# First stage of an encoder layer: only k, v and a quarter of q first, summed in PSUM, and the rest of q inside the attention

## The chip, the core and the metric

The kernel runs on one core of a Trainium2 chip. The metric is the device time of one execution in microseconds (us), median of several runs. Before the change it is 1121.42 us (three runs, 1117.03 to 1121.68). One further execution, recorded by the profiler, took 1123.08 us; its trace spans 1121.3 us from the first to the last instruction. All durations below come from that execution.

## What is computed

One layer of an encoder: 256 tokens of width 2048, everything in fp32. A vector `c` gives, by a matrix of 2048 x 12288, shifts, scales and gates; the input is scaled and shifted by them, goes through a windowed attention with 32 query heads and 8 key heads, a layer norm, and an MLP of width 8192 with a second norm.

```python
c_act = jax.nn.silu(c)
mod = c_act @ mod_w[i] + mod_b[i]
sh_m, sc_m, g_m, sh_f, sc_f, g_f = jnp.split(mod, 6, axis=-1)
hmix = x * (1.0 + sc_m[:, None, :]) + sh_m[:, None, :]
proj = hmix @ w_qkv + b_qkv                      # 2048 x 3072: q 2048, k 512, v 512
q, k = apply_rope(q, cos, sin), apply_rope(k, cos, sin)
s = where(|kpos - qpos| <= 128, q k^T / 8, -inf)
p = exp(s - m) / (sum(exp(s - m)) + exp(sink - m))
y = (p @ v) @ w_o + b_o
x = layer_norm(ALPHA * x + (1 + g_m) * y)
u = square(relu((x * (1 + sc_f) + sh_f) @ w1 + b1))
x = layer_norm(ALPHA * x + (1 + g_f) * (u @ w2 + b2))
```

## The kernel before

**Stream.** Weights come from HBM in chunks of 1 MB (128 x 2048 floats) through one list, `Stream.q`. SyncE issues the loads in the order of the list, into five buffers (`raws`) and, up to the second step of the attention, three more (`raws2`). A matrix chunk is split in two halves: ScalarE rounds each to `wh` (L281), VectorE forms the rest `wl = raw - wh` (L252). Each product of two fp32 tiles is then three matmuls (`mm3`, L560 to L562): xh wh, xh wl, xl wh. A chunk serves 24 matmuls of 128 x 512.

**Modulation.** `mod` chunks are of two kinds. A row chunk is multiplied on TensorE (`Mod.step`, L336); a column chunk is multiplied and summed in one VectorE instruction (`Col.step`, L376). A group of k tiles (`Group`) is turned into columns (`columns`, L405) and then `modulated` (L581) makes the scaled input, split into `hh` and `hl`. The first stage needs 32 such chunks, 18 rows and 14 columns. The list goes on with chunks for the gate and for the MLP's scales (`plan_late`, `SLOT_FILL`).

**First stage.** The 2048 rows of `w_qkv` are taken in six groups of 1, 1, 2, 4, 4 and 4 k tiles (`MIXG`), each over all six column chunks of 512 (k, v and four of q). Since five PSUM banks cannot hold twelve sums, `evict` (L596) copies the first partial sum to SBUF and adds each later one on VectorE (L607). `ORDER`, `CARRY` and `FIRST` are orders written out by hand. 19 of the 24 chunks of `w_qkv` are multiplied before the attention starts, five (`LATE`) in its first five steps.

**Attention.** Sixteen steps n = 0 to 15, one for each pair of key heads, half of the queries and half of the group: `scores` (L744), softmax, `normalise`, in the next step `probs_T`, every second step `values`. Each step also multiplies one matrix chunk: a late one of `w_qkv` in steps 0 to 4, from step 5 (`OUT_AT`) one of `w_o`. After step 15 five steps with a `w_o` chunk alone follow. `project` takes `w_o` in four passes over heads, each ends with an addition to `ys` on VectorE. `rope` and `heads_T` (L730) prepare the next quarter of q every fourth step. After the last chunk the norm follows (`add_gated`, `norm_scalars`, `normed`), its result is transposed (`ff_input`, L985) and the MLP starts (L1055).

**Order.** Each engine runs its instructions in a fixed order; a framework sorts them beforehand and adds the waits. `S.pin` keeps the program's order in the first stage. PSUM's eight banks are in three pools: five for sums, two for transposes, one for row chunks.

Of the kernel before, what the change touches and what calls it, by code (L numbers as in the profile page):

```python
# [20 lines left out]
S = 256  # L21
# [20 lines left out]
FIRST = [[(0, 0), (0, 1), (0, 2), (0, 3)],  # L42
         [(0, 4), (0, 5), (1, 4), (1, 5)],
         [(1, 0), (1, 1), (1, 3), (1, 2)]]
# [27 lines left out]
def hybrid_kernel(ctx: ExitStack, tc: tile.TileContext, a, out: bass.AP):  # L72
# [7 lines left out]
    psa = ctx.enter_context(tc.tile_pool(name="psa", bufs=5, space=PSUM))  # L80
    pst = ctx.enter_context(tc.tile_pool(name="pst", bufs=2, space=PSUM))
    psm = ctx.enter_context(tc.tile_pool(name="psm", bufs=1, space=PSUM))
# [48 lines left out]
    def spread():  # L131

        for c in range(4):
            ps = psa.tile([128, 512], F32, name="pa")
# [184 lines left out]
    class Mod:  # L319
# [24 lines left out]
        def step(self, raw):  # L344
            w, kc, i = self.w, self.kc, self.i
            if i == 0:
                self.ps = psm.tile([128, 512], F32, name="pm")
# [31 lines left out]
    class Group:  # L379
# [25 lines left out]
        def columns(self):  # L405
# [8 lines left out]
            pt = pst.tile([128, 512], F32, name="pt")  # L414
# [8 lines left out]
    class Gate(Group):  # L423
# [15 lines left out]
        def rows(self, m, h):  # L439
            pt = pst.tile([128, 512], F32, name="pt")  # L440
# [9 lines left out]
        def spread(self, g):  # L450
# [3 lines left out]
            pt = pst.tile([128, 512], F32, name="pt")  # L454
# [21 lines left out]

    G = len(MIXG)
    LATE = [(5, 3), (4, 4), (5, 4), (4, 5), (5, 5)]

    ORDER = {2: (1, 0, 2), 3: (5, 4, 3, 0, 2, 1), 4: (1, 2, 3, 0), 5: (0, 1, 2)}  # L480
    CARRY = {((1, 2), 2), ((2, 2), 5), ((3, 1), 1), ((4, 0), 0)}
    CARRY |= {(x, x[1]) for x, y in zip(LATE, LATE[1:]) if x[1] == y[1]}
    qk_order = [(g, c) for g in range(2, G) for c in ORDER[g]]
    wq = lambda g, c: S.plan(a["wqkv"][m_mix[g].k0 * 6 // 4 + c])
    m_mix[0].plan(2)
    S.plan(a["wqkv"][0])
    m_mix[1].plan(2)
    S.plan(a["wqkv"][1])
    S.plan(a["wqkv"][2])

    S.side[len(S.q)] = lambda: load_x(1)
    m_mix[2].plan(3)
    wq(2, ORDER[2][0])
    m_mix[2].plan(1)
    for g in range(2, G):
        n = len(ORDER[g])
        if g + 1 < G:
            S.side[len(S.q)] = lambda g=g: load_x(g)
        for x, c in enumerate(ORDER[g][1:], 1):
            if g + 1 < G:  # L500
                m_mix[g + 1].plan({2: [0, 0, 3], 3: [0, 2, 2, 2, 1, 1], 4: [0, 3, 3, 2]}[g][x])
            wq(g, c)
        if g == 2:
            m_mix[3].plan(4)
        if g + 1 < G:
            wq(g + 1, ORDER[g + 1][0])
        if g == 2:
            m_mix[3].plan(1)
# [10 lines left out]
    OUTS = [(c, js, x) for js in ((0,), (1,), (2,), (3,)) for c in range(4) for x in range(len(js))]  # L519
    for n in range(OUT_AT + 16):  # L520
        plan_late(SLOT_FILL[n])
        if n == X_AT:
            S.side[len(S.q)] = lambda: load_rows()
        if n < len(LATE):
            wq(*LATE[n])
# [55 lines left out]
    def modulated(g):  # L581
        m = m_mix[g]
        m.columns()
        k0, nk = m.k0, m.nk
        hh, hl = g4(F32R), g4(F32R)
        for k in range(nk):
            s = slice(k * 256, k * 256 + 256)
            xt, sc, sh = xts.pop(k0 + k), modm[:, 0, k0 + k:k0 + k + 1], modm[:, 1, k0 + k:k0 + k + 1]
            tc.keep_in_program_order(nc.scalar.activation(hh[:, s], xt, AF.Identity, scale=sc, bias=sh))  # L589
            tc.keep_in_program_order(nc.vector.tensor_scalar(xt, xt, sc, sh, op0=OP.mult, op1=OP.add))  # L590
            tc.keep_in_program_order(nc.vector.tensor_sub(hl[:, s], xt, f32(hh[:, s])))  # L591
        held[g] = hh, hl
# [3 lines left out]
    def evict(c, pss):  # L596

        new = c not in acc
        if new:
            acc[c] = g4()  # L600
        for t in range(NT):
            av = acc[c][:, t * 512:t * 512 + 512]
            if new:
                bq(pss[t], c)
                nc.scalar.copy(av, pss[t])
            else:
                nc.vector.tensor_add(av, av, pss[t])  # L607

    def banks():
        return [psa.tile([128, 512], F32, name="pa") for _ in range(NT)]  # L610

    def qkv_first(n):

        wh, wl = S.main()
        for i, (g, p) in enumerate(FIRST[n]):
            hh, hl = held[g]
            c = CORD[p]
            opens = c not in half
            held_back = ((g, n), p) in CARRY or (n == 1 and g == 0)
            pss = half.pop(c, None) or banks()  # L620
            for t in range(NT):
                s = slice(t * 128, t * 128 + 128)
                mm3(pss[t], hh[:, s], hl[:, s], wh(i), wl(i), opens, c in acc and not held_back)
            if i % 2:
                S.done()
            if held_back:
                half[c] = pss
            else:
                evict(c, pss)
# [623 lines left out]
```

## Time and profile before

| what | us |
| --- | --- |
| median of three runs | 1121.42 |
| profiled execution | 1123.08 |
| its span | 1121.3 |
| first matmul of the first `scores` | 170.24 |
| first matmul of the last `scores` (step 15) | 325.98 |
| last `mm3` of the attention starts | 369.81 |
| first matmul of the MLP (L1055) | 384.26 |
| TensorE / VectorE / ScalarE busy, share of the span | 96% / 71% / 47% |

Busy is not the same as fast: a matmul of 128 x 512 is listed with 0.39 us, while the next one starts 0.23 us after it. How much of a stage is lost is therefore seen from starts and from the idle times that the timeline puts in brackets, with what ended them. The granted clock is 1.0 at full speed and 0.5 when the chip throttles TensorE.

### The profile page before, as it was taken

How to read it: one execution, taken by the hardware profiler on the slowest of the kernel's cores; microseconds unless marked ns; L12 is line 12 of the kernel's file. 1: busy time of each engine (PE TensorE's matmuls, PEld its weight loads, DVE VectorE, ACT ScalarE, POOL GpSimd, SP SyncE). 2: the span in 40 equal slices, each digit the busy share in tenths (PEclk: the TensorE clock that was granted, in tenths of full speed). 3: DMA queues.
4: the chain of work that ended last, by engine and by line, in shares of the span. 5: the costliest groups of instructions: out<-in, count | busy, mean ns of one | idle time of the engine just before them, and what ended most of it. 6: DMA issues, size and time to landing. Idle time of an engine off the chain costs nothing.

```text
span 1121.3 us, 16337 instructions
## 1 busy us (share of the span) xinstructions
PE 1071.7 (96%) x6554; PEld 884.6 (79%) x6554; DVE 799.9 (71%) x1157; ACT 526.8 (47%) x811; POOL 20.3 (2%) x40
## 2 busy tenths in 40 slices
PE   8699999999999699999999999999999999999995
PEld 6578766667777499988888887888888888888884
DVE  2797898887879866765568886766665656665576
ACT  4433337766763445653345543344444434444340
POOL 1000000000000000000000000000000000000001
PEclk9999999998999799999999999999999999999998
DMA  9999998785876788555678787876555555557521
GB/s 384 425 425 427 411 371 338 293 298 198 316 285 226 305 325 326 175 186 191 229 281 294 261 291 251 309 287 218 186 184 192 200 188 188 188 187 264 188 75 75
DMA packets 43652, 292.75 MB, mean 261 GB/s; under 512 B 4876, under 2 KB 5036, under 8 KB 9784
## 3 DMA queue, kind: packets, MB, share of 16 engines
q1 hardware_dynamic: 40400, 281.96, 67.4%
q0 software_dynamic: 2432, 8.41, 2.5%
q10 hardware_dynamic: 744, 1.34, 0.3%
q8 instruction: 51, 0.84, 0.3%
q14 instruction: 25, 0.20, 0.1%
HBM read 289.57 MB, written 2.11 MB: 260 GB/s over the span
## 4 chain that ended last, share of the span: by engine, by line
PE 83%; DVE 8%; DMA 4%; issue 3%; ACT 2%; SPq 0%; POOL 0%; DVEq 0%; POOLq 0%; ACTq 0%
PE pa L1079 16%; PE pa L560 15%; PE pa L561 14%; PE pa L562 14%; PE pa L1080 8%; PE pa L1056 3%; PE pa L1057 3%; PE pa L1055 3%; DMA raw<-in_mod 3%; PE pm L336 3%; DVE raw L376 2%; DVE wl L252 2%; PE pa L753 1%; ACT wh L281 1%; PE pt L792 1%
## 5 line engine op out<-in xcount | busy, mean ns | idle before, releaser
L252 DVE TENSOR_TENSOR wl<-raw,wh 128x1024 fp32r<-128x1024 f32 x332 | 403.0, 1223 | 225.3 <-ACT wh L281 222.7
L281 ACT CAST wh<-raw 128x1024 fp32r<-128x1024 f32 x332 | 347.6, 1050 | 440.3 <-PE pa L562 240.0
L560 PE MATMUL pa<-wh,g 128*128 128x512 f32 x816 | 324.6, 399 | 4.8 <-ACT g L589 2.1
L561 PE MATMUL pa<-wl,g 128*128 128x512 f32 x816 | 321.3, 394 | 2.1 <-DVE wl L252 2.1
L562 PE MATMUL pa<-wh,g 128*128 128x512 f32 x816 | 319.5, 393 | 1.9 <-DVE g L591 1.4
L1079 PE MATMUL pa<-g,wh 128*128 128x512 f32 x768 | 271.6, 399 | 0.0
L1080 PE MATMUL pa<-g,wl 128*128 128x256 f32 x768 | 215.7, 281 | 0.0
L560 PEld LDWEIGHTS pa<-wh,g 128*128 128x128 f32 x816 | 154.4, 189 | 45.5 <-issue 6.2
L562 PEld LDWEIGHTS pa<-wh,g 128*128 128x128 f32 x816 | 154.4, 189 | 36.5 <-DVE g L591 3.0
L561 PEld LDWEIGHTS pa<-wl,g 128*128 128x128 f32 x816 | 154.7, 190 | 35.5 <-DVE wl L252 3.3
L1079 PEld LDWEIGHTS pa<-g,wh 128*128 128x128 f32 x768 | 144.3, 188 | 36.2 <-issue 0.2
L1080 PEld LDWEIGHTS pa<-g,wl 128*128 128x128 f32 x768 | 145.1, 189 | 0.1
L376 DVE CUSTOM_DVE_ANT_0 raw<-raw,cb 128x2048 f32<-128x2048 f32 x54 | 123.4, 2286 | 19.8 <-DMA raw<-in_mod 19.8
L1056 PE MATMUL pa<-g,wh 128*128 128x256 f32 x256 | 73.7, 288 | 0.4 <-DVE g L999 0.4
L1055 PE MATMUL pa<-g,wh 128*128 128x256 f32 x256 | 73.3, 289 | 0.3 <-ACT g L991 0.3
L1057 PE MATMUL pa<-g,wl 128*128 128x256 f32 x256 | 73.1, 286 | 0.0
L336 PE MATMUL pm<-raw,cact 128*32 128x128 f32 (+1 forms) x1216 | 46.5, 289 | 6.0 <-DMA raw<-in_mod 5.7
L1055 PEld LDWEIGHTS pa<-g,wh 128*128 128x128 f32 x256 | 49.8, 196 | 1.1 <-ACT g L991 0.7
L1056 PEld LDWEIGHTS pa<-g,wh 128*128 128x128 f32 x256 | 49.7, 194 | 1.1 <-DVE g L999 0.7
L1057 PEld LDWEIGHTS pa<-g,wl 128*128 128x128 f32 x256 | 49.8, 194 | 0.2 <-issue 0.2
L336 PEld LDWEIGHTS pm<-raw,cact 128*32 128x32 f32 x1216 | 31.7, 110 | 21.6 <-issue 11.2
L770 ACT ACTIVATE g<-g,nm 128x256 f32<-128x256 f32 x64 | 31.8, 498 | 21.3 <-DVE nm L760 21.3
(174 smaller groups left out, 696.4 us busy)
## 6 DMA issues: line engine op xcount, KB each, us to landing
raw<-in_mod SPq DMA_DIRECT2D x96, 1024.0 KB, 7.7
raw<-in_w SPq DMA_DIRECT2D x64, 1024.0 KB, 4.9
raw<-in_w1b SPq DMA_DIRECT2D x48, 1024.0 KB, 4.9
raw<-in_wqkv SPq DMA_DIRECT2D x24, 1024.0 KB, 10.9
raw<-in_wo SPq DMA_DIRECT2D x16, 1024.0 KB, 6.0
raw<-in_w1a SPq DMA_DIRECT2D x16, 1024.0 KB, 7.6
g<-in_x SPq DMA_DIRECT2D x4, 512.0 KB, 7.0
gb<-in_lnrow POOLq DMA_DIRECT2D x8, 256.0 KB, 6.0
```

The lines of the kernel that those rows point to most:

```text
L252: self.pinned(nc.vector.tensor_sub(l, r, f32(self.hs[n])))
L281: self.pinned(nc.scalar.copy(h, s))
L336: i = nc.tensor.matmul(self.ps[32 * j:32 * j + 32, :w], lhsT[j] if type(lhsT) is list else lhsT, rhs[j], start=self.first, stop=stop)
L376: S.pinned(nc.vector.tensor_tensor_reduce(out=raw, in0=raw, in1=cb, scale=1.0, scalar=0.0, op0=OP.mult, op1=OP.add, accum_out=self.dst))
L560: nc.tensor.matmul(ps, xh, wh, start=start, stop=False)
L561: nc.tensor.matmul(ps, xh, wl, start=False, stop=False)
L562: S.prev = nc.tensor.matmul(ps, xl, wh, start=False, stop=stop).ins
L1055: nc.tensor.matmul(o, wh(w, 128), hh, start=new, stop=False)
L1056: nc.tensor.matmul(o, wh(w, 128), hl, start=False, stop=False)
L1057: nc.tensor.matmul(o, wl(w, 128), hh, start=False, stop=end)
L1079: nc.tensor.matmul(ps, wh(k, 128), hb, start=k == 0, stop=False)
L1080: nc.tensor.matmul(ps[:, :256], wl(k, 128), hb[:, :256], start=False, stop=k == NK - 1)
```

## The change

- **Modulation by single k tiles.** `MIXG` is sixteen groups of one. Tiles 0, 1, 2 and all even ones come from row chunks, the others from column chunks: again 18 rows and 14 columns.
- **First stage.** `units` takes w_qkv tile by tile, each k tile over three column chunks only: k, a quarter of q, v. Six PSUM banks (`sums`) hold the six sums over all sixteen tiles. That is 12 chunks of `w_qkv` with the 32 of `mod`; 44 chunks in place of 51 stand ahead of the attention's own. The scaled tiles of a chunk are made while the chunk before it is multiplied (`AHEAD`).
- **Late chunks.** The other three quarters of q are twelve chunks, four k tiles each, with the two sums of a quarter kept in PSUM over four chunks (`half`). Three are multiplied ahead of step 0, with the rotation of k and q between them, nine in steps 0 to 8. `w_o` starts at step 9, so nine steps without `scores` follow step 15 where five did.
- **Evictions.** `evict` is one ScalarE copy; the additions on VectorE are gone. A bias matmul for each sum stays.
- **w_o** in two passes over two head quarters each (`OUTS`), so `project` adds to `ys` half as often.
- **Buffers.** One PSUM pool of eight banks. The three extra buffers are given up after the first stage; from step 3 late tiles of q use their space. The gate's rows lie in `g4` tiles, filled by the same transfers of GpSimd's queue one step later; `SLOT_FILL` spreads the same 34 chunks over 28 steps in place of 21, none in the last three. The rows of x are loaded at step 15 in place of 10, and `project_0(3)` runs at step 20 in place of 16.

```diff
-OUT_AT = 5
-X_AT = 10
-SLOT_FILL = (2, 2, 2, 2, 2, 2, 2, 2, 1, 1, 1, 1, 1, 2, 2, 2, 2, 2, 2, 1, 0)
-MIXG = (1, 1, 2, 4, 4, 4)
-MIXP = (1, 1, 1, 2, 2, 2)
+PRE = 3
+OUT_AT = 9
+X_AT = 15
+SLOT_FILL = (1, 1, 1, 1, 2, 1, 2, 1, 2, 1, 2, 1, 1, 1, 1, 1, 1, 1, 1, 1, 2, 2, 2, 2, 2, 0, 0, 0)
+MIXG = (1,) * 16
+MIXP = tuple(int(k < 3 or k % 2 == 0) for k in range(16))
...
+UNITS = [(k, p) for k in range(NK) for p in range(3)]
...
+    LATE = [(g, p) for p in (3, 4, 5) for g in range(4)]
+    CARRY = {(x, x[1]) for x in LATE if x[0] < 3}
...
     def evict(c, pss):
-        new = c not in acc
-        if new:
-            acc[c] = g4()
+        acc[c] = (g4b if late_tiles else g4)()
         for t in range(NT):
-            av = acc[c][:, t * 512:t * 512 + 512]
-            if new:
-                bq(pss[t], c)
-                nc.scalar.copy(av, pss[t])
-            else:
-                nc.vector.tensor_add(av, av, pss[t])
+            bq(pss[t], c)
+            nc.scalar.copy(acc[c][:, t * 512:t * 512 + 512], pss[t])
...
+    sums = [banks() for _ in range(3)]
+
+    def units(n):
+        wh, wl = S.main()
+        for i in range(4):
+            k, p = UNITS[4 * n + i]
+            hh, hl = held[k // 4]
+            for t in range(NT):
+                s = slice(k % 4 * 256 + t * 128, k % 4 * 256 + t * 128 + 128)
+                mm3(sums[p][t], hh[:, s], hl[:, s], wh(i), wl(i), k == 0, False)
+            if k == NK - 1:
+                evict(CORD[p], sums[p])
+            if i % 2:
+                S.done()
+            yield
...
-    OUTS = [(c, js, x) for js in ((0,), (1,), (2,), (3,)) for c in range(4) for x in range(len(js))]
+    OUTS = [(c, js, x) for js in ((0, 1), (2, 3)) for c in range(4) for x in range(2)]
...
     kA = whole(rope(4, 0))
-    run(qkv(G - 1, 1))
-    kT = heads_T(kA)
+    run(qkv(*LATE[0]))
     qA[0] = whole(rope(0, 1))
-    run(qkv(G - 1, 2), [lambda: qT.__setitem__(0, heads_T(qA[0]))])
+    kT = []
+    run(qkv(*LATE[1]), [lambda: kT.append(heads_T(kA))])
+    kT = kT[0]
+    run(qkv(*LATE[2]), [lambda: qT.__setitem__(0, heads_T(qA[0]))])
```

How the fixed orders change, at three places. First VectorE at the end of the first stage, where k is rotated (L717 to L722, after the change L679 to L684; `colm` is a column chunk of the gate). Before:

```order
L607 TENSOR_TENSOR g_295<-g_295,pa 128x512
L376 ISA raw,colm<-raw,cb 128x2048
L376 ISA colm 128x1
L607 TENSOR_TENSOR g_295<-g_295,pa 128x512
L717 TENSOR_TENSOR g_1426<-g_295,trig 128x16x32 x2
L720 TENSOR_TENSOR g_295<-g_295,trig 128x16x32 x2
L252 TENSOR_TENSOR wl<-raw,wh 128x1024
L722 TENSOR_TENSOR g_295<-g_295,g_1426 128x1024
```

Of the change, at the same place:

```order
L252 TENSOR_TENSOR wl<-raw,wh 128x1024 x2
L376 ISA raw,colm<-raw,cb 128x2048
L376 ISA colm 128x1
L679 TENSOR_TENSOR g_1142<-g_1115,trig 128x16x32 x2
L682 TENSOR_TENSOR g_1115<-g_1115,trig 128x16x32 x2
L252 TENSOR_TENSOR wl<-raw,wh 128x1024
L684 TENSOR_TENSOR g_1115<-g_1115,g_1142 128x1024
```

The two additions of partial sums are gone; the rotation still stands behind a column chunk, and the second `wl` of the first late chunk stands behind most of the rotation.

Second TensorE in step 7, where the third quarter of q is transposed (`heads_T`: L738, after the change L700) ahead of the scores of step 8 (L753, now L715; the rows between are `mm3`). Before:

```order
L560 MATMUL pa<-wh,g_1821 128x512
L561 MATMUL pa<-wl,g_1821 128x512
L562 MATMUL pa<-wh,g_1822 128x512
L738 MATMUL pt<-ident,g_462 128x128 x8
L753 MATMUL pa<-g_1483,g_2336 128x256 x4
L560 MATMUL pa<-wh,g_1821 128x512
```

Of the change, at the same place, up to the first three of twelve `mm3` rows:

```order
L754 MATMUL pt<-ident,g_1909 128x128 x8
L700 MATMUL pt<-ident,g4b 128x128 x8
L542 MATMUL pa<-wh,g_727 128x512
L543 MATMUL pa<-wl,g_727 128x512
L544 MATMUL pa<-wh,g_728 128x512
```

and the end of those twelve:

```order
L542 MATMUL pa<-wh,g_727 128x512
L543 MATMUL pa<-wl,g_727 128x512
L544 MATMUL pa<-wh,g_728 128x512
L715 MATMUL pa<-g_1262,g_2074 128x256 x4
L542 MATMUL pa<-wh,g_943 128x512
```

Twelve matmuls now stand between the transposes and the scores that read them.

Third VectorE at the end of the attention (`add_gated` L817 to L819, now L779 to L781; `norm_scalars` from L823, now L785; `wl` here is of the MLP's first chunks). Before, both halves of the tokens go together:

```order
L376 ISA raw,modf<-raw,cb 128x2048
L376 ISA modf 128x1
L817 TENSOR_TENSOR tmp<-pa,g4b 128x512 x2
L818 TENSOR_TENSOR g_2154<-g_2154,tmp 128x512 x2
L819 BN_STATS st_2909<-g_2154 128x6
L819 BN_STATS st_2910<-g_2154 128x6
L823 BN_AGGR mv<-st_2909 128x2
```

Of the change:

```order
L779 TENSOR_TENSOR tmp<-pa,g_2698 128x512
L780 TENSOR_TENSOR g_2397<-g_2397,tmp 128x512
L252 TENSOR_TENSOR wl<-raw,wh 128x1024
L781 BN_STATS st_2707<-g_2397 128x6
L252 TENSOR_TENSOR wl<-raw,wh 128x1024
L785 BN_AGGR mv<-st_2707 128x2
L779 TENSOR_TENSOR tmp<-pa,g_2698 128x512
L787 TENSOR_SCALAR ve<-mv 128x1
L421 TENSOR_TENSOR modf<-pt,pack 128x2x2
L780 TENSOR_TENSOR g_2397<-g_2397,tmp 128x512
```

The first half of the tokens goes ahead of the second, with two `wl` between its instructions.

More of the change, by code (lines that the diff above doesn't have):

```diff
@@ L609, in banks @@
     def banks():
-        return [psa.tile([128, 512], F32, name="pa") for _ in range(NT)]
-    def qkv_first(n):
+        return [bank() for _ in range(NT)]
+    sums = [banks() for _ in range(3)]
+    def units(n):
         wh, wl = S.main()
[L615 to L620, printed above, removed]
+        for i in range(4):
+            k, p = UNITS[4 * n + i]
+            hh, hl = held[k // 4]
@@ L1096, in ff_out @@
     def ff_out(blk, us, c):
-        pss = [psa.tile([128, 512], F32, name="pa") for _ in range(NT)]
+        pss = [bank() for _ in range(NT)]
         for kg in range(4):
```

217 lines of the change are left out of this document (87 added, 130 removed).

## The prediction

> **What bounds the kernel now.** I read the busy times by stage first, then the timeline of TensorE at the borders of the stages, then the groups of the attention. The stages are cut at the first and the last scores, at the end of the attention's last matmul and at the MLP's first:
>
> ```profile
> core 0: us, PE busy (x) PEld busy (x) DVE busy (x) ACT busy (x) POOL busy (x), PEclk, DMA share, GB/s
> 0.00:19.60 19.60, 14.45 (x149) 12.21 (x149) 4.30 (x13) 8.71 (x13) 4.96 (x16) 1.00 0.91 366
> 19.60:60.00 40.40, 31.55 (x274) 23.75 (x271) 29.74 (x48) 19.07 (x30) 0.00 (x0) 0.89 1.01 425
> 60.00:160.00 100.00, 97.55 (x704) 75.46 (x702) 87.17 (x114) 36.52 (x44) 0.00 (x0) 0.99 1.01 420
> 160.00:170.24 10.24, 6.74 (x49) 4.92 (x48) 10.24 (x13) 3.61 (x6) 0.00 (x0) 1.00 0.78 290
> 170.24:325.98 155.74, 152.02 (x1068) 109.08 (x1069) 125.86 (x272) 108.17 (x266) 2.81 (x5) 0.97 0.78 291
> 325.98:370.20 44.22, 42.10 (x273) 32.66 (x275) 41.05 (x66) 16.81 (x32) 1.06 (x2) 1.00 0.62 216
> 370.20:384.26 14.06, 3.88 (x55) 2.55 (x55) 11.87 (x31) 7.33 (x11) 0.00 (x0) 0.69 1.02 422
> 384.26:1121.30 737.04, 723.46 (x3997) 624.01 (x3997) 489.64 (x607) 326.59 (x412) 11.49 (x17) 0.99 0.62 221
> ```
>
> TensorE is busy almost throughout; up to 160 us the DMA engines are full as well (share 1.01). So two resources are balanced in the first stage, and from there on TensorE alone has the say. What the change can win is the time in which TensorE does nothing, some 8 us up to 60 us (31.55 of 40.40), 3.5 before the scores, under 4 in the attention, 10 at its end. Its work stays: same matrices, same row chunks. The price of one matmul is the distance of starts, here 21 of them in 4.76 us, 0.227 us; a chunk of 24 is 5.45 us. A row chunk is 1.08 us:
>
> ```profile
> 357.24 0.39 PE L560 MATMUL pa<-wh,g 128*128 128x512 f32 x1
> ...
> 362.00 0.39 PE L560 MATMUL pa<-wh,g 128*128 128x512 f32 x1
> ...
> 12.91 1.08 PE L336 MATMUL pm<-raw,cact 128*32 128x128 f32 x32
> ```
>
> **Step A, up to the first scores (now 170.24).** Before, 19 chunks of w_qkv are multiplied ahead of it, now 15, which takes 4 x 5.45 = 21.8 us of work away. But the work can't be pulled together freely: 12 chunks with 32 of mod must land first. The eleventh chunk of the stream is cast here as soon as it lands:
>
> ```profile
> 33.39 1.05 ACT L281 CAST wh<-raw 128x1024 fp32r<-128x1024 f32 x1 [0.53 <-DMA raw<-in_wqkv]
> ...
> GB/s 384 425 425 427 411 371 338 293 298 198 316 285 226 305 325 326 175 186 191 229 281 294 261 291 251 309 287 218 186 184 192 200 188 188 188 187 264 188 75 75
> ```
>
> By then 11 x 1.0486 + 0.66 (x, bias, constants) = 12.2 MB have come. The last chunk of the new first stage is the 44th; with all of x that is 48.4 MB, 36.2 MB more, at 425 GB/s 85.2 us: it lands at 118.6. A cast (1.05) and a difference (1.22) later, near 121.1, its remaining 23 matmuls run, 5.2 us, and six bias matmuls 1.4: 127.7. Three row chunks 3.2, three late chunks 16.4, sixteen transposes of k and q some 2: 149.3. In this stretch VectorE does the rotations and the late `wl`; their prices:
>
> ```profile
> L252 DVE TENSOR_TENSOR wl<-raw,wh 128x1024 fp32r<-128x1024 f32 x49 | 58.5, 1220 | 9.8 <-ACT wh L281 9.7
> ...
> L376 DVE CUSTOM_DVE_ANT_0 raw<-raw,cb 128x2048 f32<-128x2048 f32 x20 | 45.7, 2285 | 1.5 <-DMA raw<-in_mod 1.5
> ...
> L717 DVE TENSOR_TENSOR g<-g,trig 128x512 f32<-128x512 f32 x6 | 3.8, 682 | 0.0
> ```
>
> The sum of k leaves PSUM near 124.5; behind it on VectorE stand a `wl`, a column chunk, four rotation products and the second `wl` of the first late chunk, 1.22 + 2.29 + 4 x 0.68 + 1.22, the first of them not before its cast at 125.5: done near 133.1, where TensorE wants it at 131.3. That is a new wait of 1.8 us, and **A is 151**, 19 us sooner. Bounds: 146 if the wait and half the small ones vanish, 158 by the second rival.
>
> The old end of this stage had a wait too: the transposes of k stood 3.26 us for VectorE, and the clock dropped after it.
>
> ```profile
> 164.61 1.07 PE L336 MATMUL pm<-raw,cact 128*32 128x256 f32 x16
> 168.94 1.06 PE L738 MATMUL pt<-ident,g 128*128 128x128 f32 x8 [3.26 <-DVE g L722]
> 170.24 1.72 PE L753 MATMUL pa<-g,g 64*128 64x256 f32 x8 [0.24 <-ACT g L739]
> ```
>
> This one goes, since a late chunk now runs while k is rotated; the wait for `wl` is what is late next.
>
> **Step B, fifteen steps between first and last scores (now 155.74).** One chunk per step before and after.
>
> ```profile
> L560 PE MATMUL pa<-wh,g 128*128 128x512 f32 x120 | 51.7, 431 | 0.6 <-DVE nm L760 0.5
> ...
> L376 DVE CUSTOM_DVE_ANT_0 raw<-raw,cb 128x2048 f32<-128x2048 f32 x14 | 32.0, 2286 | 4.0 <-DMA raw<-in_mod 4.0
> ...
> L336 PE MATMUL pm<-raw,cact 128*32 128x128 f32 (+1 forms) x336 | 14.0, 302 | 0.0
> ...
> L889 DVE TENSOR_TENSOR g4b<-g4b,pa 128x512 f32<-128x512 f32 x10 | 6.8, 683 | 4.9 <-PE pa L562 4.9
> L887 DVE TENSOR_TENSOR g4b<-pa,g4b 128x512 f32<-128x512 f32 x8 | 5.5, 688 | 2.9 <-PE pa L562 2.9
> L607 DVE TENSOR_TENSOR g<-g,pa 128x512 f32<-128x512 f32 x8 | 5.4, 684 | 3.1 <-PE pa L562 3.1
> ```
>
> TensorE's list here loses three row chunks (13 to 10, to the steps after), 3.2 us, and gains six bias matmuls, 1.4. VectorE loses about four column chunks (9 us), and of the 26 additions of the last three rows some 18 (12 us). But VectorE is busy 126 of 156 us, TensorE 152: relief of an engine that isn't the bound pays only where TensorE waited for it. One such place is seen, in step 7:
>
> ```profile
> 249.65 1.14 PE L738 MATMUL pt<-ident,g 128*128 128x128 f32 x8 [0.25 <-ACT g L794]
> 253.16 2.08 PE L753 MATMUL pa<-g,g 64*128 64x256 f32 x8 [2.37 <-ACT g L739]
> ...
> 250.00:255.00 5.00, 2.63 (x15) 1.68 (x13) 3.94 (x5) 3.59 (x8) 0.00 (x0) 0.76 0.75 242
> 255.00:260.00 5.00, 5.00 (x15) 3.79 (x14) 2.21 (x11) 2.68 (x10) 0.00 (x0) 0.56 0.39 164
> ```
>
> The scores stood right behind the transposes, waited 2.37 us, and the clock fell to half for what comes to 1.2 + 2.2 us lost. Twelve matmuls (2.7 us) now fill the wait. In step 3, though, only two matmuls and a row chunk stand there, and the rotated q is later; I count 2 of the 5 to 6 us as won. **B is 155.7 - 3.2 + 1.4 - 2 = 152**; bounds 147 (all small waits gone too) and 157 (none gone, and a wait as in step 7 at a new place).
>
> **Step C, from the last scores to the MLP (now 58.3).** Ten chunks in place of six: 54.5 us of matmuls, scores, transposes and values 5.7 as now (the 42.1 busy of that stage less six chunks, 32.7, and the row chunks in it, an estimate of 3.5 at 1.08 each, 3.7), four row chunks 4.3, waits 1.5: 66. VectorE has in these 66 us 20 `wl`, 5 column chunks and 8 passes of norm additions, about 51, and is late by little. Then the end:
>
> ```profile
> 369.81 0.39 PE L562 MATMUL pa<-wh,g 128*128 128x512 f32 x1
> ...
> 375.91 1.23 DVE L252 TENSOR_TENSOR wl<-raw,wh 128x1024 fp32r<-128x1024 f32 x1 [1.90 <-ACT wh L281]
> ...
> 378.15 2.29 DVE L376 CUSTOM_DVE_ANT_0 raw<-raw,cb 128x2048 f32<-128x2048 f32 x1
> ...
> 380.96 0.69 PE L985 MATMUL pt<-ident,g 128*128 128x128 f32 x2 [8.45 <-DVE g L848]
> ...
> 384.26 1.01 PE L1055 MATMUL pa<-g,wh 128*128 128x256 f32 x3 [0.32 <-ACT g L991]
> ...
> L894 DVE BATCH_NORM_STATS2 st<-g 128x6 f32<-128x512 f32 x6 | 3.9, 683 | 0.0
> ...
> L846 ACT ACTIVATE g<-g,nmr,r 128x512 f32<-128x512 f32 x4 | 3.0, 803 | 0.8 <-DVE nmr L843 0.8
> L848 DVE TENSOR_SCALAR g<-g,mv,r 128x512 f32<-128x512 f32 x4 | 2.1, 543 | 0.0
> ```
>
> Now it takes 14.1 us. VectorE's list after the change, from the first half's `add_gated` to the last scalar of the second half: six additions and statistics 4.1, four `wl` 4.9, a column chunk 2.3, four normalisations 2.2, some twenty small ones 2.8, together 16.3. The first half stands ready 5.5 us before the second, but VectorE comes from its backlog only about 1.8 us before the end of the matmuls, so 14.5 remain, and a normalisation on ScalarE (0.8), transposes and the first scaled tile 0.7 follow: 16. The idle 1.90 for the first MLP chunk goes, since its buffer is freed by a column chunk well before; two `wl` in the chain take its place. **C is 82**; bounds 79 (no backlog) and 88 (that chunk late after all).
>
> **The sum.** The MLP (737.0) isn't touched. 151 + 152 + 82 + 737 = 1122, against a span of 1121.3: +0.7 us. The execution was 1.8 us longer than its span and 1.7 above the median of the runs, so against the median the forecast is **1122 us, no change that can be measured**. What the DMA stage gives back by starting 19 us sooner is paid by four more chunks, 21.8 us, after the attention.
>
> **Rivals.** (1) *VectorE was the hidden brake*: all its small delays go. Then A is 148, B 147, C 79.5, in all 9.8 us less, 1112. For it: VectorE is full (10.24 of 10.24, 41.05 of 44.22) just before the two borders, and loses over 30 us of additions in all. Against it: TensorE's own idle time in B is under 4 us.
>
> (2) *The clock in the first stage*, slower. TensorE now waits for data in every chunk. Per k tile it needs three units of 1.37 and row chunks of 1.2 on average, 5.3 us, while 2.75 chunks at 2.46 us land in 6.8. It is harmless while the mean granted clock is above 5.3 / 6.8 = 0.78; below, the stage falls behind. At 0.73 it loses 0.5 us on each of some 14 tiles, A is 158 and the time 1129. For it: the waits of 2.37 and 3.26 us above were both followed by half clock (0.56 in the five us after the first). Against it: row chunks and small matmuls cut the waits; one of 1.43 us left the clock alone:
>
> ```profile
> 29.05 0.50 PE L560 MATMUL pa<-wh,g 128*128 128x512 f32 x1 [1.43 <-ACT g L605]
> ```
>
> The Trainium skill, "TensorE: Matmul & The Clock Gate", section "HAM oscillation — how this bites in real kernels", warns of just such kernels: a wait for data in every tile that is longer than about 3.4 us makes every tile start cold. By that figure alone no wait here, cut into pieces of 2 to 3 us, would count, and A would stay at 151; the trace disagrees, since 2.37 us sufficed, and by it some would.
>
> (3) *The first MLP chunk comes late*, and the square root waits behind its cast on ScalarE as it does now: C is 88, time 1128.
>
> (4) That the change doesn't do what it says: the first stage isn't held by DMA since buffers come free late. Then A grows as in (2); it is counted there.
>
> **Chances.** Forecast 0.44, (1) 0.30, (2) with (4) 0.17, (3) 0.09. A measurement of this kernel tells about 0.5% (5.6 us) from no change: faster 0.30, same 0.44, slower 0.26. The forecast's own range is 1116 to 1128; with most of (1) and of (2) and (3) it is 1109 to 1132.
>
> **What will show it.** First scores at 151 with DMA share 1.0 up to 118; clock above 0.8 in that stage; steps of 10.1 us; the last scores at 303, the MLP at 385. A first `scores` after 156 with a clock below 0.78 is rival 2; steps under 9.8 us are rival 1. The forecast is wrong if the waits inside the steps, which I can see only as sums, are of another kind than in step 7.

## The result, and the profile after

The changed kernel takes 1130.51 us (median of four runs, 1128.43 to 1130.84), the kernel before, measured beside it, 1119.64. The ratio is 1.0094, with a 95% interval of 1.0065 to 1.0124: slower by 0.9%, clear of noise, where the forecast had no change that can be measured (1122, range 1109 to 1132; it gave slower a chance of 0.26). The execution that was profiled took 1130.56 us, its span is 1128.8.

The stages of the changed kernel, cut at the same events as before, in a view of windows (length, busy time of each engine, granted clock, DMA share, GB/s):

```profile
core 0: us, PE busy (x) PEld busy (x) DVE busy (x) ACT busy (x) POOL busy (x), PEclk, DMA share, GB/s
19.60:141.20 121.60, 95.01 (x803) 71.20 (x802) 74.88 (x110) 33.79 (x49) 0.00 (x0) 0.87 0.97 394
141.20:168.40 27.20, 26.34 (x156) 19.41 (x154) 22.98 (x24) 14.14 (x19) 1.23 (x2) 1.00 0.81 291
168.40:313.40 145.00, 143.68 (x979) 105.70 (x979) 110.41 (x248) 111.67 (x273) 2.10 (x4) 1.00 0.78 286
313.40:377.50 64.10, 64.10 (x410) 51.23 (x408) 55.02 (x77) 26.31 (x41) 0.53 (x1) 1.00 0.88 338
377.50:392.25 14.75, 5.24 (x108) 4.05 (x106) 10.87 (x31) 6.57 (x11) 0.00 (x0) 0.78 0.90 361
392.25:1128.80 736.55, 724.12 (x3997) 624.42 (x3997) 488.28 (x604) 325.79 (x411) 11.51 (x17) 0.99 0.62 219
```

| stage | before | forecast | measured | miss |
| --- | --- | --- | --- | --- |
| A, up to the first scores | 170.2 | 151 | 168.4 | +17.4 |
| B, first to last scores | 155.7 | 152 | 145.0 | -7.0 |
| C, last scores to the MLP | 58.3 | 82 | 78.9 | -3.1 |
| D, the MLP | 737.0 | 737 | 736.6 | -0.4 |

The sum (1122 against the span of 1128.8) missed by 6.9 us because one miss of 17.4 was set off by two others of 10.1. A time inside the range says little for the reasoning here. In the first stage TensorE is busy 95.0 of 121.6 us, and the group of the second matmul shows what it waited for: `wl`, 21.9 us of idle time in the whole execution, 21.1 of them in six waits between 15 and 150 us (next, the group's row on the page: count, busy time and mean, then the idle time ahead and its releaser).

```profile
L543 PE MATMUL pa<-wl,g 128*128 128x512 f32 x816 | 323.4, 396 | 22.0 <-DVE wl L252 21.9
```

One such wait, in the timeline (start, duration, engine, line; the idle time ahead in brackets):

```profile
113.48 0.32 PE L416 MATMUL pt<-both,mrow 128*128 128x2 f32 x2
113.84 0.16 DVE L421 TENSOR_TENSOR modm<-pt,pack 128x2 f32<-128x2 f32 x1 [6.07 <-PE pt L416]
114.04 0.60 ACT L570 ACTIVATE g<-g,modm 128x256 fp32r<-128x256 f32 x1 [0.67 <-DVE modm L421]
114.54 1.98 ACT L281 CAST wh<-raw 128x1024 fp32r<-128x1024 f32 x2
115.12 0.43 DVE L572 TENSOR_TENSOR g<-g,g 128x256 fp32r<-128x256 f32 x1
115.46 2.28 DVE L376 CUSTOM_DVE_ANT_0 raw<-raw,cb 128x2048 f32<-128x2048 f32 x1
115.62 0.80 PE L542 MATMUL pa<-wh,g 128*128 128x512 f32 x2 [1.82 <-ACT wh L281]
117.67 2.29 DVE L376 CUSTOM_DVE_ANT_0 raw<-raw,cb 128x2048 f32<-128x2048 f32 x1
120.08 1.22 DVE L252 TENSOR_TENSOR wl<-raw,wh 128x1024 fp32r<-128x1024 f32 x1
121.35 0.79 PE L543 MATMUL pa<-wl,g 128*128 128x512 f32 x1 [4.93 <-DVE wl L252]
```

Read from the top: TensorE finishes the row of tile 12 (L416); VectorE, which had idled 6.07 us for it, makes tile 12, and only then, since its list is fixed, takes the two column chunks of tile 13, and only then `wl` of the next matrix chunk, whose first half had been cast by 115.6. No transfer appears in this chain. Behind the wait stands a row of 0.79 us, half clock (such a row takes 0.39 at full clock). The chain is as long as its instructions, 7.9 us from L416 to L543, whatever the data do.

### The profile page after: what moved, and what is told of

It is laid out like the page before. It is cut to its first block, busy times and chain, and to the rows that moved or that the text cites. A ratio compares the mean times of both kernels' runs of the same rounds, so it can differ in the third digit from the quotient of the medians.

```text
span 1128.8 us, 16294 instructions
## 1 busy us (share of the span) xinstructions
PE 1072.6 (95%) x6563; PEld 887.9 (79%) x6563; DVE 766.7 (68%) x1103; ACT 526.9 (47%) x814; POOL 20.4 (2%) x40
## 4 chain that ended last, share of the span: by engine, by line
PE 86%; DVE 9%; ACT 3%; issue 1%; DMA 1%; DVEq 0%; ACTq 0%
PE pa L1046 16%; PE pa L543 15%; PE pa L544 15%; PE pa L542 15%; PE pa L1047 8%; DVE raw L376 4%; PE pm L336 4%; PE pa L1022 3%; PE pa L1023 3%; PE pa L1024 3%; DVE wl L252 3%; PE pa L715 1%; PE pt L754 1%; PE pa L770 1%; ACT wh L281 1%
## 5 line engine op out<-in xcount | busy, mean ns | idle before, releaser
L543 PE MATMUL pa<-wl,g 128*128 128x512 f32 x816 | 323.4, 396 | 22.0 <-DVE wl L252 21.9
L543 PEld LDWEIGHTS pa<-wl,g 128*128 128x128 f32 x816 | 155.3, 190 | 57.6 <-DVE wl L252 25.5
L1047 PEld LDWEIGHTS pa<-g,wl 128*128 128x128 f32 x768 | 145.1, 189 | 0.1
L336 PE MATMUL pm<-raw,cact 128*32 128x128 f32 (+1 forms) x1216 | 48.9, 305 | 0.0
L336 PEld LDWEIGHTS pm<-raw,cact 128*32 128x32 f32 x1216 | 34.2, 117 | 14.7 <-issue 12.1
```

The lines of the kernel that those rows point to most:

```text
L336: i = nc.tensor.matmul(self.ps[32 * j:32 * j + 32, :w], lhsT[j] if type(lhsT) is list else lhsT, rhs[j], start=self.first, stop=stop)
L543: nc.tensor.matmul(ps, xh, wl, start=False, stop=False)
L1047: nc.tensor.matmul(ps[:, :256], wl(k, 128), hb[:, :256], start=False, stop=k == NK - 1)
```

## Experiments

Two theories for stage A. **ORDER**: the fixed order of VectorE makes `wl` late, and the data would be there. **DATA**: the stage is held by transfers, as the prediction's sum had it, only later. **CLOCK**, rival 2 of the prediction, says that the half clock behind the waits is the price. For stage B, **FILL** (the wait of step 7 and the half clock are gone) stands against **RELIEF** (VectorE has less to do, rival 1). The stage times below are of one profiled execution each, medians and ratios of the timed runs; the interval of each ratio is in the table at the end of this section.

### Row and column tiles swapped in three pairs

```diff
-MIXP = tuple(int(k < 3 or k % 2 == 0) for k in range(16))
+MIXP = tuple(int(k == 0 or k % 4 in (1, 2)) for k in range(16))
```

> Reference points of the changed kernel: first scores at 168.4, and in its first stage TensorE waits 5.00, 5.82, 3.15 and 4.93 us for `wl`. Three of these (at 49, 85 and 116 us) follow chunks during which two k tiles are modulated, the row tile first, then the column tile, so that VectorE reaches the second tile's column chunks only after the first tile's row came through TensorE, and the next `wl` stands behind both. Here those pairs are swapped: the column tile first, the row tile second (same counts of rows and columns). Theory ORDER (the fixed order of VectorE costs the time, data are there): these three waits fall below 1.5 us each, the half clock behind them goes too, first scores at 155 to 161, time 1118 to 1124. Theory DATA (the stage is held by the transfers or by buffers that come free late for another reason): each wait comes back as one for a cast or a transfer, first scores at 166 or later, time 1128 to 1131. Theory CLOCK (the waits are covered, only the half clock behind them costs): like ORDER, but the gain is no more than 6 us.

Measured: first scores at 153.7 (14.7 sooner), 1119.08 us, level with the kernel before: sooner than the 155 to 161 of ORDER, and more than the 6 us that CLOCK allowed. At the three places TensorE now waits 0.94 us at most, and for a row or the cast; the longest waits left are the 5.82 us treated next and one of 2.48 us at the end. And the first stage has a new limit: its last chunk is cast as soon as it has landed. The timeline of this kernel, then the same cast in the changed one:

```profile
118.32 2.00 ACT L281 CAST wh<-raw 128x1024 fp32r<-128x1024 f32 x2 [3.54 <-DMA raw<-in_wqkv]
```

```profile
128.30 0.27 ACT L365 COPY mrow<-pm 128x128 f32<-128x128 f32 x1 [7.51 <-PE pm L336]
128.47 2.00 ACT L281 CAST wh<-raw 128x1024 fp32r<-128x1024 f32 x2
```

In the changed kernel ScalarE waited 7.51 us for TensorE's row ahead of this cast, not for a transfer. ORDER holds; the last chunk landed within 0.3 us of the prediction's 118.6 once nothing else was later.

### Sines and cosines early, alone and with the swap

```diff
     idle(8)
+    trig = rotary_tables()
     S.pin = True
...
-        if n == 2:
-            trig = rotary_tables()
```

The wait that it aims at, in the changed kernel (the first and the last of VectorE's instructions for the tables, the cast, and who waited):

```profile
64.50 0.38 DVE L157 TENSOR_SCALAR g<-pack,posf 128x32 f32<-128x32 f32 x2
...
67.26 1.98 ACT L281 CAST wh<-raw 128x1024 fp32r<-128x1024 f32 x2
67.39 0.26 DVE L176 TENSOR_SCALAR trig<-trig 128x192 f32<-128x192 f32 x1 [0.22 <-ACT trig L174]
68.83 0.80 PE L543 MATMUL pa<-wl,g 128*128 128x512 f32 x1 [5.82 <-DVE wl L252]
```

> The sines and cosines (13 instructions of VectorE, 64.5 to 67.6 us, and one loading of a table on ScalarE) are made before the first weights are needed instead of between chunk 3 and 4 of w_qkv. ORDER: the wait of 5.82 us at 61.6 us falls to 2 or less, and the half clock behind it goes; first scores 4 to 7 us sooner (161 to 165), time 1124 to 1127. DATA: the wait turns into one for a transfer, first scores within 1.5 us of 168.4, time 1129 to 1131. CLOCK: sooner by 1 to 3 us.

> The two edits together that each shortened the first stage of the changed kernel: the pairs of row and column tile swapped (first scores 153.7 instead of 168.4) and the sines and cosines made early (164.4). With the swap alone the longest wait left is the one of 5.82 us behind the sines and cosines, at 56 us. ORDER: the two gains add up, 14.7 and 4.0: first scores at 149 to 151, time 1113 to 1116, faster than the kernel before. DATA: below the 151 that the transfers allow by the prediction's sum nothing is to be had, and the wait comes back as one for a cast: first scores at 152 to 154, time 1117 to 1119.

Measured alone: first scores at 164.4 (4.0 sooner), 1126.11 us, as ORDER has it. This kernel repeats one round of 31.6 us from one wait of 5.00 us to the next. In the round from 80.6 us on VectorE idles 5.42 and 5.16 us for rows from TensorE, and 0.7 at most for ScalarE, never for a transfer; between the last two of these waits the transfers run at 394 GB/s, below the 425 before the change, though the DMA share reads 1.00:

```profile
86.53:118.14 31.61, 24.52 (x204) 17.71 (x204) 19.59 (x27) 8.50 (x12) 0.00 (x0) 0.88 1.00 394
```

Together: 154.6 and 1116.05. The two gains don't add up: the last cast is at the same place as with the swap alone, behind a transfer. So DATA holds up to this cast (420 to 430 GB/s in each ten us from 20 to 130); what stands behind it is treated further down.

```profile
118.43 2.00 ACT L281 CAST wh<-raw 128x1024 fp32r<-128x1024 f32 x2 [2.63 <-DMA raw<-in_wqkv]
...
123.65 0.50 PE L543 MATMUL pa<-wl,g 128*128 128x512 f32 x1 [2.71 <-DVE wl L252]
```

The 3 us between the medians of the two kernels with the swap are not shown to be a gain: they ran on different chips, the intervals of their ratios to the kernel before overlap, and stage A is 0.9 us longer with both. The profile of the swap alone (1115.16 us) was its fastest execution, that of both (1118.16) its slowest.

### Filling the waits with zeros

```diff
+    def fill(n):
+        for _ in range({3: 18, 6: 24, 9: 24}.get(n, 0)):
+            tc.keep_in_program_order(nc.tensor.matmul(
+                sums[UNITS[4 * n][1]][0], identr, zero[:, None, :].to_broadcast([128, 16, 32]), start=False, stop=False))
...
         wh, wl = S.main()
+        fill(n)
```

> Matmuls with zeros (18, 20, 10 and 18 of 0.23 us) are put on TensorE ahead of chunks 3, 4, 6 and 9, so that it is busy for most of each of the four waits for `wl`; nothing else moves, and the waits end no sooner by themselves. CLOCK: the half clock at 54.9, 68.8, 89.6 and 121.4 us goes, first scores 5 to 9 us sooner, time 1121 to 1125. ORDER: the half clock goes too, but it lay mostly in time that the loop over VectorE would have waited anyway; first scores within 3 us of 168.4, time 1127 to 1131.

> The filling with zeros once more, without the flaw of the first (there the 20 matmuls ahead of chunk 4 stood behind the wait and not in it, and were work on top). Base is the kernel with early sines and cosines (first scores 164.4, time 1126.1): three equal rounds with waits of 5.0 us at chunks 3, 6 and 9, each followed by half clock (54 to 59, 87 to 90, 118 to 120 us as far as single rows show it). 18, 24 and 24 matmuls with zeros now lie in these waits. CLOCK: the half clock goes, each round gets 2 to 3 us shorter (31.6 us between chunk 6 and 9 falls to 29), first scores at 156 to 160, time 1119 to 1122. ORDER: the waits alone are the price, since `wl` comes at the same distance from the row that VectorE waits for; first scores at 163 to 166, time 1125 to 1128.

The diff is of the second try, on the kernel with early tables; the first, on the changed kernel, had 18, 20, 10 and 18 matmuls ahead of chunks 3, 4, 6 and 9. Its numbers (1130.54 us, first scores at 167.7) are where ORDER put them, but they say nothing by themselves: its 20 matmuls ahead of chunk 4 came behind the wait they should have filled. The second try is clean. Windows of the same 31.6 us, one round between the pairs of tiles, first with early tables, then with the fill; below them, of the second kernel, the fill and the first column chunk on VectorE at both ends of the round:

```profile
80.79:112.41 31.62, 24.52 (x205) 17.71 (x205) 19.60 (x27) 8.51 (x13) 0.00 (x0) 0.89 1.01 406
```

```profile
80.80:112.40 31.60, 28.87 (x232) 21.48 (x231) 20.14 (x27) 9.08 (x13) 0.00 (x0) 1.00 1.01 420
```

```profile
79.83 5.91 PE L592 MATMUL pa<-zero,identr 128*128 128x512 f32 x24
80.61 2.28 DVE L376 CUSTOM_DVE_ANT_0 raw<-raw,cb 128x2048 f32<-128x2048 f32 x1
...
102.95 0.50 PE L543 MATMUL pa<-wl,g 128*128 128x512 f32 x1 [2.66 <-DVE wl L252]
...
111.65 2.29 DVE L376 CUSTOM_DVE_ANT_0 raw<-raw,cb 128x2048 f32<-128x2048 f32 x1
```

The clock is 1.00 in the round in place of 0.89, and the round still takes 111.65 - 80.61 = 31.0 us on VectorE in place of 31.6. The faster matmuls turn up as a longer wait for `wl` inside the round (2.66 us, 1.30 without the fill). First scores are at 164.7, the time is 1126.90 against 1126.11. CLOCK falls: half clock costs 0.6 us in this round, and nothing that shows in the first scores.

### A control: other tiles swapped

```diff
-MIXP = tuple(int(k < 3 or k % 2 == 0) for k in range(16))
+MIXP = tuple(int(k in (0, 1, 2, 4, 7, 8, 11, 12, 15)) for k in range(16))
```

> A control for the swap of rows and columns: the changed kernel with the tiles swapped that are modulated alone during a chunk or in no such pair (3 stays, 6 and 7, 10 and 11, 14 and 15 change places: as many of both kinds), while the three pairs 4 and 5, 8 and 9, 12 and 13 stay row first, column second. ORDER at the pairs: the three waits of 3 to 5 us for `wl` stay, first scores 165 to 171, time 1127 to 1133. If any mixing of kinds would do (the gain of the first swap was from the sequence of kinds as a whole): first scores below 162, time below 1125.

A miss: the three waits stay (4.58, 3.15 and 4.25 us), as ORDER said, but first scores come at 156.5 and the time is 1123.53. So the waits at the pairs alone are not the whole cause. With early tables a round of the changed kernel had waits of 5.00, 1.30 and 0.78 us and 31.6 us in all; here the two smaller ones are gone or down to 0.15 us, the 5.82 us behind the sines and cosines are down to 1.80 (behind two column chunks that follow them), and the last round takes 28.0 us with the transfers at 426 GB/s:

```profile
83.56:111.53 27.97, 23.56 (x201) 18.35 (x201) 19.75 (x28) 9.78 (x14) 0.00 (x0) 0.87 1.01 426
```

My reading: a round has to lose only 3 to 4 us, it doesn't matter from which wait, until the transfers hold it, since eleven chunks of 1.0486 MB and 0.52 MB of x at 425 GB/s are 28.4 us (an estimate from the rate before the change). That the lists of instructions set the round is shown; that it is the pairs alone is refuted.

### The last tile, and a version that is faster than both

The wait of 2.71 us behind the last cast above comes from a column chunk of tile 15. Making tile 15 a row (and tile 1 a column), with pairs swapped and tables early:

```diff
+MIXP = tuple(int(k in (0, 2, 5, 6, 9, 10, 13, 14, 15)) for k in range(16))
```

> As e6 (pairs swapped, sines and cosines early), and tile 15 becomes a row, tile 1 a column, so that no column chunk stands ahead of the last `wl` of the first stage. In e6 the last cast comes at 118.4, behind a transfer, and after it TensorE waits 2.71 us for `wl` and runs at half clock from 124.7 to 127.6. ORDER: wait and half clock go, first scores at 149 to 152 instead of 154.6, time 1112 to 1115. If the transfers decide this end too (the last chunk can't be multiplied sooner): first scores at 153.5 to 155, time 1115 to 1117.

First scores at 150.9, as ORDER has it and where the forecast's sum was (151); k's sum leaves PSUM at 125.4 (forecast 124.5). But the time is 1117.65, outside the 1112 to 1115 expected, because stage B is 148.5 where it was 145.0. A wait for a row of the gate in step 4 is longer, and half clock follows it. The changed kernel first, then this one:

```profile
216.20 0.44 PE L444 MATMUL pt<-ident,mrow 128*128 128x128 f32 x2 [1.32 <-ACT mrow L442]
216.48 1.04 PE L754 MATMUL pt<-ident,g 128*128 128x128 f32 x8
217.44 1.95 PE L770 MATMUL pa<-g,g 128*64 128x256 f32 x16
```

```profile
200.57 0.44 PE L444 MATMUL pt<-ident,mrow 128*128 128x128 f32 x2 [2.94 <-ACT mrow L442]
200.84 1.85 PE L753 MATMUL pt<-ident,g 128*128 128x128 f32 x8
202.62 2.76 PE L769 MATMUL pa<-g,g 128*64 128x256 f32 x16
```

The wait costs 1.6 us more, the two rows behind it 1.6, another wait 0.35: about the 3.5 us (the granted clock is 0.89 over the 15 us from 195.9 on, 1.00 throughout in the changed kernel). The control above, where tile 15 is a row too, has the same wait of 2.94 and a B of 148.3.

The second edit is at the other end. It makes the first four `wl` of the MLP wait on VectorE for the first scaled tile:

```diff
-            self.pinned(nc.vector.tensor_sub(l, r, f32(self.hs[n])))
+            i = nc.vector.tensor_sub(l, r, f32(self.hs[n]))
+            self.pinned(i)
+            if self.hold:
+                tc.add_manual_dep(i.ins, self.hold.pop().name, ORDER_ONLY, reason="behind")
...
-                nc.vector.tensor_sub(hl, hf[:, s], f32(hh))
+                i = nc.vector.tensor_sub(hl, hf[:, s], f32(hh))
+                if k == 0:
+                    S.hold = [i.ins] * 4
```

> As v1, and at the end of the attention the first four `wl` of the MLP (four times 1.22 us) are held on VectorE until the first scaled tile of the MLP is made; in the changed kernel two of them stand between the norm's instructions and two ahead of the first scaled tile. If VectorE's list sets the transition (as the prediction's sum has it), it falls from 14.6 to 11 to 12.5 us, time 2 to 3.5 us below v1. If the square root on ScalarE or the late `wl` itself sets it: 14 to 15 us, or TensorE waits for `wl` behind the first matmuls of the MLP, and the time is within 1 us of v1.

Measured: from the last `mm3` to the MLP 11.4 us in place of 14.6, time 1112.93, 4.7 below the kernel without the second edit (expected 2 to 3.5; the transition explains 3.2), ratio to the kernel before 0.9947 (0.9930 to 0.9964). The transposes of the norm's result in the changed kernel, and in this one:

```profile
384.35 0.44 PE L952 MATMUL pt<-ident,g 128*128 128x128 f32 x2 [3.60 <-DVE g L810]
390.38 1.54 PE L952 MATMUL pt<-ident,g 128*128 128x128 f32 x6 [5.59 <-ACT g L808]
```

```profile
367.78 0.44 PE L955 MATMUL pt<-ident,g 128*128 128x128 f32 x2 [1.23 <-DVE ve L790]
373.06 1.54 PE L955 MATMUL pt<-ident,g 128*128 128x128 f32 x6 [4.28 <-ACT g L811]
```

Both waits are shorter, so the list of VectorE had its part in the transition, as the prediction's sum of step C had it. But the edit also moved the square root of the second half on ScalarE. In the changed kernel its input is ready at 383.4, and it stands behind a cast that waits for a transfer; in this one it comes ahead of that cast:

```profile
384.64 1.04 ACT L281 CAST wh<-raw 128x1024 fp32r<-128x1024 f32 x1 [4.82 <-DMA raw<-in_w1a]
385.59 0.20 ACT L789 ACTIVATE sd<-ve 128x1 f32<-128x1 f32 x1
385.82 0.17 DVE L791 RECIPROCAL r<-sd 128x1 f32<-128x1 f32 x1 [1.07 <-ACT sd L789]
```

```profile
367.82 0.20 ACT L792 ACTIVATE sd<-ve 128x1 f32<-128x1 f32 x1 [2.43 <-DVE ve L790]
370.30 1.99 ACT L285 CAST wh<-raw 128x1024 fp32r<-128x1024 f32 x2 [2.28 <-DMA raw<-in_w1a]
```

Against the kernel without the second edit, whose cast comes late too (4.33 us), the square root's input is ready 2.2 us sooner, and the square root starts at once instead of 1.4 us later. What each would have been worth alone isn't separated.

### Stage B: wait or load

Four kernels. The transposes of q after the whole chunk instead of in its middle:

```diff
-                mid.append(lambda: qT.__setitem__(j + 1, heads_T(qA[j + 1])))
...
         next(w, None)
+        if j < 3 and i == 3:
+            qT[j + 1] = heads_T(qA[j + 1])
```

> The transposes of the next quarter of q are issued after the whole chunk of steps 3, 7 and 11 instead of in its middle; four or no matmuls stand between them and the scores, where the changed kernel has twelve. The fifteen steps between first and last scores take 145.0 us in the changed kernel and 155.7 before. Theory FILL (the gain of the steps is the wait of 2.37 us in step 7 and the two stretches of half clock that are gone): a wait of 1 to 2.4 us comes back in at least one of the steps 3, 7 and 11, with half clock where it is over 2; steps 147 to 153 us, time 1132 to 1138. Theory RELIEF (the gain comes from VectorE, which lost some 30 instructions): steps within 1.5 us of 145, time 1129 to 1132.

B is 146.2, 1131.90 us in all. Both lie where RELIEF put them, but they don't decide: no wait of the old kind came back, for a reason of its own. In the kernel before, ScalarE's copies of the transposes, which the scores read, stood behind a cast and the four instructions of `normalise` (249.98 to 252.53 us); here `normalise` is done when the transposes start, only a cast stands ahead, and in step 7 three matmuls cover it. So the twelve matmuls between transposes and scores are not needed in every order. Load alone, 30 instructions of VectorE:

```diff
+        if n < 15:
+            for _ in range(2):
+                tc.keep_in_program_order(nc.vector.tensor_tensor(cb[:, :512], cb[:, :512], cb[:, :512], op=OP.max))
```

> Steps 0 to 14 of the changed kernel each get two instructions of VectorE more (128 x 512 elements, 0.68 us each, some 20 us in all; `cb` is replaced by the larger of itself and itself), so VectorE is as full between first and last scores as in the kernel before (126 of 156 us there, 110 of 145 in the changed one). RELIEF: steps 150 to 156, time 1135 to 1142. FILL: steps 144 to 148, time 1129 to 1134.

```profile
168.70:313.94 145.24, 144.03 (x979) 105.58 (x979) 125.97 (x277) 111.37 (x274) 2.10 (x4) 1.00 0.78 284
```

VectorE is busy 126.0 us, as much as before the change, and the steps take 145.2: RELIEF falls for stage B, as far as it means load as such (here at the end of each step). The opposite test is on the kernel before, the scores of step 8 behind the first half of its chunk:

```diff
-        if n < 16:
+        if n < 16 and n != 8:
             scores(n)
...
         next(w, None)
+        if n == 8:
+            scores(n)
```

> The kernel before with one edit: the scores of step 8 come behind the first half of that step's chunk, so that twelve or more matmuls stand between the transposes of step 7 and the scores that read them, as in the changed kernel. FILL: the wait of 2.37 us and the half clock from 253 to 259 us go, nothing takes their place: first to last scores 150 to 152 us instead of 155.7, time 1113.5 to 1116 against 1118.7. RELIEF (VectorE is the brake, the wait is only where it shows): the wait comes back elsewhere, time 1117 to 1120.

```profile
249.83 1.03 PE L738 MATMUL pt<-ident,g 128*128 128x128 f32 x8
...
253.32 1.13 PE L753 MATMUL pa<-g,g 64*128 64x256 f32 x8
```

The scores have no idle time in brackets any more and take 1.13 us instead of 2.08. B falls from 155.7 to 149.6, the time to 1113.80 against 1117.66 in the same runs: the one wait and its half clock were worth 6.2 us of the profiled stage, 3.9 us by the medians. The profiled execution of the kernel before (1123.08 us) was a slow one for that kernel, so the medians are the safer figure. Last, w_o in four passes again:

```diff
-    OUTS = [(c, js, x) for js in ((0, 1), (2, 3)) for c in range(4) for x in range(2)]
+    OUTS = [(c, js, x) for js in ((0,), (1,), (2,), (3,)) for c in range(4) for x in range(len(js))]
```

> w_o goes in four passes over one quarter of the heads each, as in the kernel before, so that VectorE has 16 additions of 0.68 us more in the steps from 9 on; all else is the changed kernel (145.0 us between first and last scores, 78.9 from there to the MLP, 1130.5 in all). FILL (VectorE's load doesn't matter): steps 144 to 147, last part 78 to 81, time 1129 to 1133. RELIEF: steps 148 to 151 or the last part 82 or more, time 1134 to 1139.

B is 145.0, but C 87.5, and the time 1135.68: some 5 us slower. So four passes cost time in stage C only, 8.6 us in this profile (the slowest execution of this kernel, 1138.21). The rows where it begins, in the last scores:

```profile
310.63 2.29 DVE L376 CUSTOM_DVE_ANT_0 raw<-raw,cb 128x2048 f32<-128x2048 f32 x1 [5.23 <-DMA raw<-in_mod]
...
315.34 0.79 PE L542 MATMUL pa<-wh,g 128*128 128x512 f32 x1 [2.30 <-DVE nm L722]
```

A column chunk whose transfer is late stands ahead of the maxima that TensorE's next matmul waits for; in the changed kernel the column chunk at this place waits 0.75 us for its transfer. How much of the 5 us is this and how much the additions themselves isn't separated.

### All runs

| kernel | median us | ratio to before (95%) | A | B | C |
| --- | --- | --- | --- | --- | --- |
| changed | 1130.51 | 1.0094 (1.0065 to 1.0124) | 168.4 | 145.0 | 78.9 |
| pairs swapped | 1119.08 | 0.9993 (0.9975 to 1.0011) | 153.7 | 145.0 | 78.7 |
| tables early | 1126.11 | 1.0075 (1.0047 to 1.0102) | 164.4 | 145.0 | 78.9 |
| both | 1116.05 | 0.9977 (0.9961 to 0.9993) | 154.6 | 145.1 | 79.8 |
| zeros, first try | 1130.54 | 1.0111 (1.0080 to 1.0141) | 167.7 | 145.0 | 78.5 |
| tables early, zeros | 1126.90 | 1.0070 (1.0048 to 1.0093) | 164.7 | 145.0 | 78.6 |
| other tiles swapped | 1123.53 | 1.0039 (1.0024 to 1.0053) | 156.5 | 148.3 | 79.2 |
| both, last tile a row | 1117.65 | 0.9983 (0.9969 to 0.9998) | 150.9 | 148.5 | 78.7 |
| the same, `wl` held | 1112.93 | 0.9947 (0.9930 to 0.9964) | 151.0 | 148.5 | 75.5 |
| transposes last | 1131.90 | 1.0121 (1.0090 to 1.0152) | 168.0 | 146.2 | 79.0 |
| load on VectorE | 1130.67 | 1.0114 (1.0092 to 1.0136) | 168.7 | 145.2 | 78.8 |
| four passes of w_o | 1135.68 | 1.0159 (1.0133 to 1.0186) | 166.9 | 145.0 | 87.5 |
| before, scores 8 later | 1113.80 | 0.9960 (0.9944 to 0.9977) | 170.2 | 149.6 | 57.5 |

The last row is worth a second look: one edit to the kernel before, without the change, can't be told from the fastest version of the changed kernel (the intervals of 1113.80 and 1112.93 overlap).

## Why the prediction was right, and where it was wrong

**Step A failed.** The prediction let the first stage end with the transfers: "it lands at 118.6. A cast (1.05) and a difference (1.22) later, near 121.1, its remaining 23 matmuls run". In the changed kernel that cast is at 128.5, and k's sum leaves PSUM at 141.7 instead of 124.5. From there to the first scores it took 26.7 us, forecast 26.5: the whole miss lies ahead, and 168.4 is outside the step's own bounds of 146 and 158. What failed is the assumption that a difference comes one cast after its chunk. VectorE's list was looked at only for the end of the stage; in its middle a `wl` that TensorE waits for stands behind column chunks, and these behind a row that TensorE has to finish first. The chain over the two engines, not the data, sets the round. With the order mended, the tables early and the last tile a row, A is 150.9.

**Rival 2 had the sign and not the cause.** It gave 158 for a clock below 0.78; the clock was 0.87 and A 168. Filled waits bring the clock back to 1.00 in a round and gain 0.6 us. Rival 4 (buffers come free late) is closer: the DMA share fell to 0.97 and the rate to 394 GB/s over the stage, with 269 GB/s from 60 to 70 us, where the sines and cosines stand. But this is a result of VectorE's order (with the tables early those ten us have 425), and it was priced with rival 2's seven us.

**Step B was mis-sized.** "I count 2 of the 5 to 6 us as won" measured 6.2 on the kernel before in the profile, 3.9 by the medians. The net of row chunks and bias, 1.8, comes on top; the remaining 2.7 of the 10.7 contain the half clock right behind the first scores, which is gone as well (clock 0.66 in the five us from 170 on before, 1.00 in those from 168.4 on after), and aren't otherwise separated. The wait was the right place, its worth too small, and 145 lies below the bound of 147. The sign that the prediction gave for rival 1 came, steps under 9.8 us (9.7): rival 1, that VectorE was the brake in B, gave nearly the same number (147) for a reason that the added load refutes.

**Step C was right in the main** (78.9 for 82, just below the bound of 79). The two parts are 64.1 for 66 and 14.75 for 16; holding back four `wl`, with the square root moved, took 3.2 of the latter away. Rival 3 came in a small form, for the second chunk of the MLP and not the first: ScalarE waits 4.82 us for its transfer, the square root of the second half stands behind that cast, and VectorE idles 1.07 us for it. The prediction's sum had no such term; its 16 was large enough all the same.

**The range held by luck**, because a stage that was 17 us late and two that were together 10 us early add up to 7.

## What to carry to other kernels

When a change lets a stage run "at the rate of the transfers", write down for one full round what stands on each in-order engine ahead of the operand that the matmuls need, and add up the chain that goes from one engine to the other and back; if it is longer than the round's transfers, the stage runs at the chain. Work that is needed later (here the column chunks of a tile that the next chunk multiplies last) shouldn't stand ahead of work that is waited for; here a swap of three pairs of tiles was worth as much as the change had cost. A forecast that is near in the sum should be compared stage by stage before it is believed.

## What was not expected of the hardware

Waits of the same length are not always followed by half clock. In the kernel with early tables and zeros TensorE waits three times for 2.66 or 2.67 us, at 67, 100 and 131 us; the matmul behind the first takes 0.79 us, those behind the second keep to 0.4 us (the first of them 0.50), and behind the third half clock begins 1.3 us later.

```profile
70.42 0.79 PE L543 MATMUL pa<-wl,g 128*128 128x512 f32 x1 [2.67 <-DVE wl L252]
...
103.30 0.40 PE L544 MATMUL pa<-wh,g 128*128 128x512 f32 x1
...
134.00 0.50 PE L543 MATMUL pa<-wl,g 128*128 128x512 f32 x1 [2.67 <-DVE wl L252]
...
135.63 0.63 PE L544 MATMUL pa<-wh,g 128*128 128x512 f32 x1
```

So the length of one wait doesn't decide it here; what does, these runs don't show. The Trainium skill, "TensorE: Matmul & The Clock Gate", section "HAM oscillation — how this bites in real kernels", gives waits longer than about 3.4 us as the ones that make TensorE start cold. All three waits here were shorter, and half clock followed two of them; the measurement decides.
